# A norm weight moved behind a transposition, and four sums of squares taken in one

## Chip, core and metric

The kernel runs on one core of a Trainium2 chip. The metric is the device time of one execution in microseconds (us). Five engines work side by side, each through a queue of its own that it takes in order: TensorE (PE, with its weight loads shown apart as PEld), VectorE (DVE), ScalarE (ACT), GpSimd (POOL), and SyncE (SP), which here only starts transfers.

## What is computed

The reference is a two-layer transformer trunk over 512 tokens of width 1024. The first layer holds two sparse attentions, the second one differential attention; each layer ends in a multilayer perceptron (MLP). The change lies in the differential attention, in its head-wise norm:

```python
pd = p[:, :, 0] - lam_full * p[:, :, 1]
o = jnp.einsum('bhqs,bshe->bqhe', pd.astype(v.dtype), v)
o = rms_norm(o, subln) * (1.0 - lambda_init)
return o.reshape(B, QBLK, DIFF_HEADS * 2 * DIFF_DIM)
# rms_norm(x, g) = x * rsqrt(mean(x * x, -1) + EPS) * g
```

There are 8 heads, and `o` has 128 values for each head and token; `subln` is a vector of 128 weights that all heads share. Behind the norm an output projection takes all heads together.

## The kernel before

Everything is float32. A product of matrices is made from high and low parts: each operand is split into `hi`, its rounded copy, and `lo`, the rest, and three matmuls (L350 to L352) are added up. A helper writes the split: ACT copies the source into `hi` (L372), DVE subtracts `hi` from the source into `lo` (L373).

`odd()` is the second attention. Its tokens go through in blocks of 128, so that a unit is one head and one block: 32 units, head by head. Each passes through stages that lie some slots apart in one loop: `s0` makes scores and the softmax (DVE L514, ACT L517), `s1` and `s1b` combine the two softmaxes (POOL L1665, DVE L1671), `s2` transposes the result (PE L1681, ACT L531), and `s3` multiplies by the values (PE L1693). The last three are those of the change:

- `s3`, once all four blocks of a head have been multiplied, copies the head's 128x512 result from PSUM to SBUF (ACT L1699) and squares it block by block on ACT, each call also writing the sum of its 128 squares to a column of a small tile `ost` (L1702, the accumulator read being an instruction of its own in the trace). For head 7 this is done after each block, on 128x128, so that the output projection can follow block by block.
- `s4`, one slot later, turns the sums into a factor for each token (DVE L1710, then seven small calls, L384 to L398) and multiplies (DVE L1714): block times factor times weight, `in1=sub`, where `sub` holds the 128 weights on every partition, since the tokens lie on partitions and the weights along the free side.
- `s5`, one more slot later, transposes the blocks (PE L1724) and splits them from PSUM into `hi` and `lo` for the output projection (L372, L373).

Beside the attention, the queries and keys of the next head are projected (`proj_fill`); with head 7 the output projection of heads 0 to 3 runs as filling (`op_unit`), its result added on DVE at L738; heads 4 to 7 follow in `layer()`, with the layer norm (`ln_a_`, L665 to L704, and `ln_b_`, L713 to L724) behind each block of tokens. All this time a stream of weights is loaded and split into parts by ACT (L265) and by DVE or POOL (L266); the weights of the output projection are also multiplied by a gate row (L262, mostly POOL, 128x1024 a call).

The tile `sub` takes one of six buffers of the tag `k`, whose other five hold key tiles of the heads; behind the attention the same buffers serve for weights of the MLP. The order of the instructions on each engine is not written out by hand: `TileContext(nc, schedule_with_timeline_sim=True)` sorts them by simulated readiness, and the loop's order is the priority.

Of the kernel before, what the change touches and what calls it, by code (L numbers as in the profile page):

```python
# [9 lines left out]
F32 = mybir.dt.float32  # L10
F32R = mybir.dt.float32r
I32 = mybir.dt.int32
AF = mybir.ActivationFunctionType
ALU = mybir.AluOpType
AX = mybir.AxisListType
# [13 lines left out]
def f32(ap):  # L29
    return ap.bitcast(F32)  # L30
# [296 lines left out]
class Trunk:  # L327
# [1267 lines left out]
    def odd(self):  # L1595
        nc, a, sm, R, B, C, st, I = self.nc, self.a, self.sm, self.R, self.B, self.C, self.st, self.I
# [1 line left out]
        fill = Fill()  # L1598
        lam = self.z()
        nc.scalar.dma_start(out=lam[:, :256], in_=a["lam"].to_broadcast([128, 256]))  # L1600
        sub = self.s2("k")[:, :128]
        nc.scalar.dma_start(out=sub, in_=a["subln"].to_broadcast([128, 128]))
        lf = sm.tile([128, 4], F32, tag="lf", bufs=1, name="lf")
        self.k_low()

# [17 lines left out]
        for j in range(2):  # L1623
            nc.vector.scalar_tensor_tensor(out=lam[:, 256 + 64 * j:320 + 64 * j], in0=lam[:, 128 * j:128 * j + 64], scalar=1.0,
                                           in1=lam[:, 128 * j + 64:128 * j + 128], op0=ALU.mult, op1=ALU.mult,
                                           accum_out=lf[:, j:j + 1])
# [8 lines left out]
        Q, K, G, ot = {}, {}, {}, []  # L1635
# [49 lines left out]
        def s3(n):  # L1685
            h, i = units[n]
            if i == 0 or h == 7:
                po[h] = self.bank("o", (128, 4, 128))
            pt = pts.pop(n)
            for j in range(i + 1):  # L1690
                js, c = slice(128 * j, 128 * j + 128), 128 * (h % 4)
                v = V[h // 4][j // 2][:, 512 * (j % 2) + c:512 * (j % 2) + c + 128]
                nc.tensor.matmul(po[h][:, i], lhsT=pt[:, js], rhs=v, start=j == 0, stop=j == i)  # L1693
            if i == 3 or h == 7:
                o, sq = self.z(), self.z()
                s = sm.tile([128, 2, 4], F32, tag="ost", bufs=3, name="ost")
                i0 = i if h == 7 else 0
                c = slice(128 * i0, 128 * i + 128)
                nc.scalar.copy(out=o[:, c], in_=po[h].rearrange("p a b -> p (a b)")[:, c])  # L1699
                for i in range(i0, i + 1):  # L1700
                    c = slice(128 * i, 128 * i + 128)
                    nc.scalar.activation(out=sq[:, c], in_=o[:, c], func=AF.Square, accum_out=s[:, 0, i:i + 1])  # L1702
                O[n] = (o, s)

        def s4(n):
            h, i1 = units[n]
            i0 = i1 if h == 7 else 0
            o, s = O[n]
            r = slice(i0, i1 + 1)
            nc.vector.tensor_scalar(out=s[:, 0, r], in0=s[:, 0, r], scalar1=1.0 / 128, scalar2=EPS, op0=ALU.mult, op1=ALU.add)  # L1710
            self.rsqrt(s[:, 1, r], s[:, 0, r], i1 + 1 - i0)
            for i in range(i0, i1 + 1):
                c = slice(128 * i, 128 * i + 128)
                nc.vector.scalar_tensor_tensor(out=o[:, c], in0=o[:, c], scalar=s[:, 1, i:i + 1], in1=sub,  # L1714
                                               op0=ALU.mult, op1=ALU.mult)

        def s5(n):
            h, i1 = units[n]
            i0 = i1 if h == 7 else 0
            o, _ = O.pop(n)  # L1720
            t = self.bank("t")
            for i in range(i0, i1 + 1):
                c = slice(128 * i, 128 * i + 128)
                nc.tensor.transpose(t[:, c], o[:, c], self.ident)  # L1724
            if len(ot) == h:
                ot.append([self.ot() for _ in range(2)])
            c = slice(128 * i0, 128 * i1 + 128)
            self.split(ot[h][0][:, c], ot[h][1][:, c], t[:, c])

        add_proj(0)  # L1730
        fill.flush()
# [3 lines left out]
        for n in range(N + 6):  # L1735
# [12 lines left out]
            if n - 5 in O:  # L1748
                s4(n - 5)
# [4 lines left out]
            if n >= 4 and n - 4 < N:  # L1754
                s3(n - 4)
# [3 lines left out]
            if n - 6 in O:  # L1759
                s5(n - 6)  # L1760
# [93 lines left out]
def onehot(dist):  # L1854
    o = np.zeros((33, len(dist)), np.float32)
    o[np.where(dist < 0, 32, buckets(dist)), np.arange(len(dist))] = 1.0
    return o


def layout(i):  # L1860
    c = np.ascontiguousarray
    i = {k: np.asarray(v) for k, v in i.items()}
    f = {}
    f["x"] = c(i["x"][0])
    f["xT"] = c(i["x"][0].T.reshape(8, 128, 512))
    f["c"] = c(i["c"])
    f["ident"] = np.eye(128, dtype=np.float32)
    rb = i["rel_bias"]
    tab = np.concatenate([rb, rb[:, NSA_SLOTS]], 1)
    f["tab"] = c(np.concatenate([tab, np.full((1, 24), NEG, np.float32)], 0))  # L1870
    dec = 512 - (16 * np.arange(NDEC)[None, :] + 15 - np.arange(16)[:, None])
    f["onehot"] = c(np.concatenate([onehot(511 - np.arange(NVEC)), onehot(dec.ravel())], 1))
    f["cT"] = c(i["c"].reshape(8, 128).T)
    f["ada_w"] = c(i["ada_w"][0, :, :5120].reshape(1024, 40, 128).transpose(1, 2, 0))
    p = i["ada_w"].reshape(2, 2, 4, 128, 24, 256).transpose(0, 4, 1, 3, 2, 5).reshape(96, 128, 1024)
    f["ada_p"] = c(p[40:])
    f["ada_b"] = c(i["ada_b"].reshape(2, 48, 128).transpose(2, 0, 1))
    f["lnc"] = c(np.stack([i["ln_g"], i["ln_b"]]).reshape(2, 4, 8, 128).transpose(3, 0, 1, 2))

    f["ln"] = c(np.stack([i["ln_g"], i["ln_b"]]).reshape(2, 4, 1024))  # L1880
    w = i["ev_w_in"][0]
    q = [w[:, 64 * h:64 * h + 64] for h in range(8)]
    kvc, kvs, kvw, gate, dq, dkv, iq, ik, iw = np.split(w[:, 512:], np.cumsum([256, 256, 256, 24, 512, 128, 512, 64]), 1)

    def b(m):
        n = m.shape[1] // 128
        return m.reshape(8, 128, n, 128).transpose(2, 1, 0, 3)

    f["ev_b1"] = c(np.concatenate([ik, ik, iq[:, :384], kvs[:, 128:], kvw[:, 128:], dkv, gate, iw], 1).reshape(8, 128, 928))
    f["ev_b2"] = c(b(np.concatenate([kvc[:, 128:]] + [q[h] for h in NSA_SLOTS] +  # L1890
                                    [iq[:, 384:], kvs[:, :128], kvw[:, :128], kvc[:, :128]], 1)))
    f["ev_b3"] = c(b(dq))
    f["kv_norm"] = c(i["dsa_kv_norm"].reshape(1, 128))
    f["ukv"] = c(np.concatenate([i["dsa_w_uk"][0].reshape(128, 512), i["dsa_w_uv"][0].reshape(128, 512)], 1))
    pe = np.stack([i["nsa_pe_k"][0], i["nsa_pe_v"][0]])
    f["pe"] = c(pe.reshape(2, 2, 16, 64).transpose(1, 3, 0, 2).reshape(128, 2, 16))
    w1 = np.stack([i["nsa_w1_k"][0], i["nsa_w1_v"][0]])
    f["cmp_w1"] = c(w1.reshape(2, 2, 4, 4, 64, 256).transpose(0, 2, 1, 4, 3, 5).reshape(2, 4, 128, 1024))
    k2, v2 = (m[0].reshape(2, 128, 64).transpose(1, 0, 2) for m in (i["nsa_w2_k"], i["nsa_w2_v"]))
    f["cmp_w2"] = c(np.concatenate([np.concatenate([k2, k2], 2).reshape(128, 256), v2.reshape(128, 128)], 1))  # L1900
    wo = i["ev_w_out"][0].reshape(16, 64, 1024)
    f["ev_out"] = c(wo[NSA_SLOTS + list(range(8, 16))].reshape(8, 128, 1024))
    w = i["od_w_in"][0]
    f["od_qk"] = c(np.stack([b(w[:, :1024]), b(w[:, 1024:2048])], 1))
    f["od_v"] = c(w[:, 2048:].reshape(4, 2, 128, 2, 512).transpose(3, 0, 2, 1, 4))
    f["od_out"] = c(i["od_w_out"][0].reshape(8, 128, 1024))
    f["lam"] = c(i["diff_lam"].reshape(1, 256))
    f["subln"] = c(i["diff_subln"].reshape(1, 128))
    w = np.stack([b(i["mlp_w1"][l]) for l in range(2)])
    w, q = w[:, :6], w[:, 6:].reshape(2, 13, 2, 128, 2, 512)  # L1910
    f["mlp_wp"] = c(np.stack([np.stack([q[:, :, 0, :, 0], q[:, :, 1, :, 1]], 3), np.stack([q[:, :, 1, :, 0], q[:, :, 0, :, 1]], 3)], 2)
                    .reshape(2, 13, 2, 128, 1024))
    f["mlp_w1"] = c(w)
    f["mlp_w2"] = c(i["mlp_w2"].reshape(2, 32, 128, 1024))
    return f
# [14 lines left out]
```

## Time and profile before

| | |
|---|---|
| median of 3 runs | 1438.86 us (1437.71 to 1439.1) |
| the profiled execution | 1441.48 us, its span 1439.4 us |
| PE busy | 1338.4 us (93%) |
| DVE busy | 1141.7 us (79%) |
| ACT busy | 659.8 us (46%) |
| POOL busy | 579.8 us (40%) |
| mean granted clock of TensorE | 0.968 of full speed |

The span runs from the first to the last instruction. The second attention's units lie between some 875 and 1041 us of it; the projection and the norm behind it reach to some 1070 us, and the MLP follows. A busy share is a mean over all stages, so it doesn't say what bounds one of them; the table by stage below does. "Idle before, releaser" names what an engine last waited for. An idle engine costs nothing where another one sets the pace.

### The profile page before, as it was taken

The numbers are of one execution on the slowest core, as the hardware profiler recorded it, in microseconds if no ns is written. First come the engines' busy times: TensorE is split into PE (matmuls) and PEld (weight loads), VectorE is DVE, ScalarE is ACT, GpSimd is POOL, SyncE is SP. The second block draws the span as 40 slices with busy tenths as digits, with TensorE's granted clock in tenths as the row PEclk, the third lists the DMA queues.
The fourth block names the chain that finished last, engine by engine and source line by source line (L and its number), as shares of the span: only waits on it lengthen the run. The fifth ranks groups of instructions, "written<-read, shape, count | busy, mean of one in ns | idle before, by whom it ended". The sixth has DMA issues, their size and how long they took to land.

```text
span 1439.4 us, 22546 instructions
## 1 busy us (share of the span) xinstructions
PE 1338.4 (93%) x8286; PEld 1123.1 (78%) x8286; DVE 1141.7 (79%) x2186; ACT 659.8 (46%) x1412; POOL 579.8 (40%) x432
## 2 busy tenths in 40 slices
PE   6979799998899999999999799999979899999985
PEld 4868676676589888888887687887769789999974
DVE  7778979667569778877789925788976997888898
ACT  3555465746365423333332536776565443333321
POOL 1423577626432444444453721124164533122234
PEclk9989999899999999999999999999989999999997
DMA  9834323313731554544542442332450233323311
GB/s 353 288 116 142 116 89 118 119 58 118 263 117 46 175 191 162 183 169 161 191 161 94 144 164 88 103 103 76 152 163 6 91 100 118 106 72 117 117 59 59
DMA packets 58657, 189.52 MB, mean 132 GB/s; under 512 B 7794, under 2 KB 8498, under 8 KB 58548
## 3 DMA queue, kind: packets, MB, share of 16 engines
q1 hardware_dynamic: 55840, 184.67, 38.0%
q10 hardware_dynamic: 2708, 3.42, 0.7%
q8 instruction: 65, 1.06, 0.3%
q14 instruction: 44, 0.36, 0.1%
HBM read 178.42 MB, written 9.64 MB: 131 GB/s over the span
## 4 chain that ended last, share of the span: by engine, by line
PE 70%; DVE 19%; DMA 4%; issue 3%; ACT 2%; POOL 1%; DVEq 0%; SPq 0%; ACTq 0%; POOLq 0%
PE ps_mm L350 9%; PE ps_mm L351 9%; PE ps_mm L352 9%; PE ps_o L350 4%; PE ps_o L351 4%; PE ps_o L352 4%; PE ps_s L351 3%; PE ps_s L350 3%; PE ps_s L352 3%; PE ps_t L350 2%; PE ps_t L352 2%; PE ps_t L351 2%; PE ps_t L1486 2%; PE ps_s L504 2%; DVE u L738 2%
## 5 line engine op out<-in xcount | busy, mean ns | idle before, releaser
L350 PE MATMUL ps_mm<-hT,b 128*128 128x256 f32 (+1 forms) x560 | 188.9, 339 | 16.9 <-ACT b L265 13.2
L351 PE MATMUL ps_mm<-hT,b 128*128 128x256 f32 (+1 forms) x560 | 188.5, 337 | 5.2 <-DVE hT L724 5.1
L352 PE MATMUL ps_mm<-hT,b 128*128 128x256 f32 (+1 forms) x560 | 187.8, 336 | 1.8 <-DVE b L220 1.8
L350 PEld LDWEIGHTS ps_mm<-hT,b 128*128 128x128 f32 x560 | 107.6, 192 | 31.9 <-ACT b L265 13.2
L351 PEld LDWEIGHTS ps_mm<-hT,b 128*128 128x128 f32 x560 | 107.8, 193 | 17.8 <-DVE hT L724 5.6
L220 POOL TENSOR_TENSOR b<-s,b 128x512 fp32r<-128x512 f32 x33 | 46.6, 1415 | 184.6 <-ACT b L219 181.2
L517 ACT ACTIVATE z<-z,st 128x128 f32<-128x128 f32 (+3 forms) x160 | 89.3, 559 | 67.2 <-DVE st L514 61.3
L903 POOL TENSOR_TENSOR ot<-z,ot 128x512 fp32r<-128x512 f32 x39 | 61.3, 1573 | 142.0 <-ACT ot L902 128.4
L352 PEld LDWEIGHTS ps_mm<-hT,b 128*128 128x128 f32 x560 | 107.5, 192 | 11.4 <-DVE b L220 2.0
L350 PE MATMUL ps_o<-b,ot 128*128 128x512 f32 x251 | 101.2, 403 | 3.9 <-ACT b L265 2.2
L351 PE MATMUL ps_o<-b,ot 128*128 128x512 f32 x251 | 99.5, 397 | 3.0 <-DVE b L266 3.0
L738 DVE TENSOR_TENSOR u<-ps_o,u 128x512 f32<-128x512 f32 x121 | 82.4, 681 | 21.6 <-PE ps_o L352 21.2
L352 PE MATMUL ps_o<-b,ot 128*128 128x512 f32 x251 | 98.8, 394 | 0.0
L514 DVE CUSTOM_DVE_ANT_0 z<-ps_s,g 128x128 f32<-128x128 f32 (+3 forms) x160 | 75.0, 484 | 25.8 <-PE ps_s L505 23.6
L265 ACT CAST b<-raw 128x1024 fp32r<-128x1024 f32 (+1 forms) x62 | 64.5, 1043 | 65.9 <-issue 16.7
L266 DVE TENSOR_TENSOR b<-s,b 128x1024 fp32r<-128x1024 f32 x47 | 70.4, 1501 | 18.3 <-ACT b L265 17.9
L265 ACT CAST b<-s 128x1024 fp32r<-128x1024 f32 x47 | 49.1, 1049 | 77.6 <-DMA s<-mlp_w 18.9
L266 DVE TENSOR_TENSOR b<-raw,b 128x1024 fp32r<-128x1024 f32 (+1 forms) x42 | 56.7, 1349 | 33.1 <-ACT b L265 32.9
L350 PE MATMUL ps_s<-b,ot 128*128 128x512 f32 x181 | 72.4, 400 | 0.0
L738 DVE TENSOR_TENSOR u<-ps_s,u 128x512 f32<-128x512 f32 x87 | 59.3, 682 | 15.9 <-PE ps_s L352 15.6
L351 PE MATMUL ps_s<-b,ot 128*128 128x512 f32 x181 | 71.7, 396 | 0.0
L352 PE MATMUL ps_s<-b,ot 128*128 128x512 f32 x181 | 71.4, 394 | 0.0
(472 smaller groups left out, 4244.1 us busy)
## 6 DMA issues: line engine op xcount, KB each, us to landing
s<-mlp_w SPq DMA_DIRECT2D x55, 512.0 KB
s<-ada_p SPq DMA_DIRECT2D x39, 512.0 KB
s<-mlp_wp SPq DMA_DIRECT2D x33, 512.0 KB
raw<-ada_w SPq DMA_DIRECT2D x23, 512.0 KB
raw<-mlp_w SPq DMA_DIRECT2D x21, 512.0 KB
raw<-mlp_wp SPq DMA_DIRECT2D x19, 512.0 KB
early<-ada_w SPq DMA_DIRECT2D x17, 512.0 KB
raw<-ada_p SPq DMA_DIRECT2D x17, 512.0 KB
```

Source lines behind the costliest of these rows:

```text
L220: (nc.gpsimd if PLAN["sl"][it.l][n] else nc.vector).tensor_tensor(out=lo, in0=src, in1=f32(hi), op=ALU.subtract)
L265: nc.scalar.copy(out=hi.cols(c.start, w), in_=raw[:, c])
L266: getattr(nc, ("vector", "gpsimd")[PLAN["lo"][it.name]] if it.name in PLAN["lo"] else k.lo_engine).tensor_sub(out=lo.cols(c.start, w), in0 ...
L350: mm(ps, lhsT=l[0], rhs=r[0], start=start, stop=False)
L351: mm(ps, lhsT=l[0], rhs=r[1], start=False, stop=False)
L352: mm(ps, lhsT=l[1], rhs=r[0], start=False, stop=stop)
L504: mm(ps, lhsT=q[:, qs], rhs=k[0][:, ks], start=start, stop=False)
L514: i = nc.vector.tensor_tensor_reduce(out=z[:, :w], in0=ps, in1=bias, scale=-1.0, scalar=3e38, op0=ALU.add, op1=ALU.min, accum_out=st[:, m: ...
L517: j = nc.scalar.activation(out=z[:, :w], in_=z[:, :w], func=AF.Exp, scale=-1.0, bias=st[:, m:m + 1], accum_out=st[:, 2 + m:3 + m])
L738: self.nc.vector.tensor_add(out=u[:, sl], in0=ps, in1=u[:, sl])
L903: (nc.gpsimd if PLAN["hl"][l][f % 2] else nc.vector).tensor_tensor(out=hl[:, c0:c1], in0=r[:, c0:c1], in1=f32(hh[:, c0:c1]), op=ALU.subtract)
L1486: self.nc.tensor.transpose(t[:, 128 * j:128 * j + 128], z[:, 128 * j:128 * j + 128], self.ident)
```

## The change

The weight becomes a factor for each partition. It is loaded as a 128x1 tile of its own instead of a row on all partitions (the array that the kernel gets is reshaped to match), `s4` multiplies by the token's factor alone, and the weight is applied behind the transposition in `s5`, where the 128 positions of a head lie on partitions: ACT writes `hi` with the weight as its scale, DVE writes `lo` as source times weight minus `hi`. In `s3` the four squares with accumulators become one ACT call on 128x512 without, and DVE sums its four blocks in one reduction; for head 7, where this goes block by block, it is a call on 128x128 and a reduction to 128x1 for each.

```diff
-        sub = self.s2("k")[:, :128]
-        nc.scalar.dma_start(out=sub, in_=a["subln"].to_broadcast([128, 128]))
+        sub = sm.tile([128, 1], F32, tag="sub", bufs=1, name="sub")
+        nc.scalar.dma_start(out=sub, in_=a["subln"])
...
-                for i in range(i0, i + 1):
-                    c = slice(128 * i, 128 * i + 128)
-                    nc.scalar.activation(out=sq[:, c], in_=o[:, c], func=AF.Square, accum_out=s[:, 0, i:i + 1])
+                nc.scalar.activation(out=sq[:, c], in_=o[:, c], func=AF.Square)
+                nc.vector.reduce_sum(out=s[:, 0, i0:i + 1], in_=sq[:, c].rearrange("p (a b) -> p a b", b=128), axis=AX.X)
...
-                nc.vector.scalar_tensor_tensor(out=o[:, c], in0=o[:, c], scalar=s[:, 1, i:i + 1], in1=sub,
-                                               op0=ALU.mult, op1=ALU.mult)
+                nc.vector.tensor_scalar(out=o[:, c], in0=o[:, c], scalar1=s[:, 1, i:i + 1], scalar2=None, op0=ALU.mult)
...
-            self.split(ot[h][0][:, c], ot[h][1][:, c], t[:, c])
+            hi, lo = (x[:, c] for x in ot[h])
+            nc.scalar.activation(out=hi, in_=t[:, c], func=AF.Identity, scale=sub)
+            nc.vector.scalar_tensor_tensor(out=lo, in0=t[:, c], scalar=sub, in1=f32(hi), op0=ALU.mult, op1=ALU.subtract)
...
-    f["subln"] = c(i["diff_subln"].reshape(1, 128))
+    f["subln"] = c(i["diff_subln"].reshape(128, 1))
```

## Rows read from the trace of the kernel before

**Rows 1.** The page: its head line.

```profile
span 1439.4 us, 22546 instructions
```

**Rows 2.** Busy us by stage: length, PE, PEld, DVE, ACT, POOL, clock, DMA.

```profile
920.00:940.00 20.00, 20.00 (x109) 16.75 (x108) 16.12 (x50) 15.51 (x42) 2.46 (x4) 1.00 0.26 80
960.00:980.00 20.00, 19.73 (x109) 16.73 (x108) 16.74 (x44) 13.86 (x39) 9.89 (x8) 1.00 0.40 109
980.00:1000.00 20.00, 17.60 (x100) 14.27 (x98) 18.68 (x49) 16.04 (x51) 8.46 (x7) 1.00 0.37 105
...
1020.00:1040.00 20.00, 19.15 (x96) 14.92 (x94) 19.84 (x68) 12.35 (x27) 2.48 (x1) 1.00 0.50 171
1040.00:1060.00 20.00, 13.32 (x65) 10.84 (x65) 18.04 (x37) 12.68 (x25) 12.59 (x10) 0.95 0.39 145
1060.00:1080.00 20.00, 15.88 (x104) 15.18 (x105) 13.17 (x20) 12.78 (x31) 10.21 (x7) 0.71 0.71 207
```

**Rows 3.** Waits, 960 to 1070 us: in total, times, longest us.

```profile
PE ps_t L713 <- ACT ot L719: 7.2, 2, 6.9
...
PE ps_mm L350 <- DVE u L738: 2.9, 3, 2.1
...
PE ps_t L1724 <- DVE z L1714: 1.3, 1, 1.3
...
DVE ost L1710 <- ACT z L1702: 1.0, 2, 0.6
```

**Rows 4.** Groups by line, 880 to 1060 us: count, busy us, mean ns.

```profile
L1702 ACT ACTIVATE z<-z 128x128 f32<-128x128 f32 x32 | 9.5, 299 | 0.3
...
L1702 ACT ACTIVATION_READ_ACCUMULATOR z<-z 128x1 f32 x32 | 6.0, 187 | 0.0
...
L373 DVE TENSOR_TENSOR ot<-ps_t,ot 128x512 fp32r<-128x512 f32 x7 | 4.8, 679 | 0.5 <-ACT ot L372 0.5
```

**Rows 5.** The chain that ended last, 880 to 1090 us: start, us, what.

```profile
996.25 1.29 ACT z L1702 x8
```

**Rows 6.** Nearest to the new calls: timeline, min/median/max by line, groups by form.

```profile
283.19 0.35 DVE L1416 TENSOR_SCALAR z<-z,st,one 128x128 f32<-128x128 f32 x1
...
L1547 DVE TENSOR_SCALAR z<-z x2: 215/854/1494, 123.0 to 157.9; 128x124 f32<-128x124 f32 x2
...
L1242 DVE TENSOR_REDUCE cst<-z x8: 256/273/285, 139.7 to 232.9; 128x4 f32<-128x128 f32 x8
...
L265 ACT CAST k<-raw 128x512 fp32r<-128x512 f32 x14 | 8.7, 622 | 18.7 <-PE ps_t L351 8.9 <-issue 4.6 <-DMA raw<-mlp_w 2.4
...
L372 ACT CAST ot<-ps_t 128x128 fp32r<-128x128 f32 x4 | 0.9, 263 | 0.1
...
L719 ACT ACTIVATE ot<-ps_t,lnr 128x128 f32<-128x128 f32 x88 | 31.9, 464 | 4.3 <-PE ps_t L713 4.3
...
L373 DVE TENSOR_TENSOR ot<-ps_t,ot 128x128 fp32r<-128x128 f32 x3 | 0.8, 284 | 0.0
```

**Rows 7.** DVE in order of time, 960 to 1041 us: start, us.

```profile
972.18 1.14 DVE L1714 SCALAR_TENSOR_TENSOR z<-z,ost,k 128x128 f32<-128x128 f32 x4
...
997.56 2.39 DVE L1710 TENSOR_SCALAR ost<-ost 128x4 f32<-128x4 f32 x1 [0.60 <-ACT z L1702]
...
1009.48 3.27 DVE L1714 SCALAR_TENSOR_TENSOR z<-z,ost,k 128x128 f32<-128x128 f32 x4
...
1018.41 0.16 DVE L1710 TENSOR_SCALAR ost<-ost 128x4 f32<-128x4 f32 x1
...
1040.90 0.35 DVE L1714 SCALAR_TENSOR_TENSOR z<-z,ost,k 128x128 f32<-128x128 f32 x1
```

**Rows 8.** POOL in order of time, the same stretch.

```profile
997.57 2.36 POOL L262 TENSOR_TENSOR raw<-raw,grow 128x1024 f32<-128x1024 f32 x1
...
1009.58 2.50 POOL L262 TENSOR_TENSOR raw<-raw,grow 128x1024 f32<-128x1024 f32 x1 [0.60 <-DMA raw<-od_out]
```

**Rows 9.** ACT in order of time, 1016 to 1068 us; idle before.

```profile
1041.28 0.62 ACT L265 CAST k<-raw 128x512 fp32r<-128x512 f32 x1 [0.77 <-DVE z L1714]
```

## The prediction, made before the changed kernel was run

> **What bounds the kernel now.** I read five views, from the whole to the place. The page gives the span of the profiled execution [rows 1]. The table by stage comes next, for the stretch in which the second attention runs and ends [rows 2]: up to about 980 us TensorE (PE) is full (20.00 of 20 us, then 19.73), while VectorE (DVE) has three to four us in twenty to spare. From 980 us it turns round: DVE is busy 18.68 of 20 us, then 19.84, then 18.04, and PE falls to 13.32 between 1040 and 1060. After that PE runs at a mean granted clock of 0.71 of full speed for 20 us. So what is added to DVE before 980 us lies beside a full PE, and what is added behind it is in the way.
>
> The list of waits says for whom PE waits in 960 to 1070 us [rows 3]: 7.2 us for ScalarE's (ACT) L719, which belongs to the layer norm behind the attention; 2.9 us for DVE's L738, which empties a bank of the output projection; 1.3 us for L1714, a line that the change rewrites. DVE in turn waits 1.0 us in two places at L1710 for ACT's squares at L1702, a wait that the change moves to its new sum.
>
> The groups by line and form give the lines touched [rows 4], one line's share of the chain stands beside them [rows 5], the nearest instructions to the new ones have rows of their own [rows 6], and DVE's order of time shows a second thing [rows 7]: four calls of L1714 take 1.14 us at 972 us but 3.27 us at 1009 us, and one L1710 on 128x4 takes 2.39 us at 997.56 where it takes 0.16 at 1018.41. In both long cases GpSimd (POOL) is in a 128x1024 product at that moment [rows 8]. A DVE call that reads or writes SBUF while such a product runs can lose some 2.2 us, and where each lands is a matter of order.
>
> **The change part by part.**
>
> The squares. Per head 0 to 6 ACT loses four L1702 calls of 299 ns with four accumulator reads of 187 ns [rows 4]. They overlap: the eight fill 1.29 us in the chain of waits [rows 5]. It gains one 128x512 square without accumulator. No row shows it; the nearest is ACT's 128x512 cast from SBUF at 622 ns [rows 6], and I take that. ACT frees about 0.7 us for each head. ACT has 12 to 16 of 20 us in this stretch [rows 2], so I count the freed time at nothing; it counts only in the latency of the chain, below.
>
> The sum. DVE gains one 128x512 to 128x4 reduction for each of seven heads, and a 128x128 to 128x1 one for each of the four units of head 7. The small one has a near row, 273 ns for 128x128 to 128x4 [rows 6]. For the large one I add the slope between DVE's 128x128 and 128x512 forms of L373, 284 and 679 ns [rows 4, 6]: 0.27 + 0.40 = 0.67 us. If it ran at two elements a cycle, the slope would be halved: 0.47. Calls in a row overlap by 0.08 us (four of 0.35 fill 1.14 [rows 7]), so in line it is 0.59 (0.39 to 0.67), and 0.19 (up to 0.27) for the small one.
>
> The normalisation. Thirty-two L1714 calls with two tensors become tensor-times-scalar calls with one. A clean L1714 takes 0.35 us [rows 7]. The nearest rows for the new one are L1416, 128x128 with two per-partition scalars, 0.35 us, and L1547, 128x124 with constants, 0.215 us at its shortest [rows 6]. The new call has one scalar, so I take the middle, 0.28. That saves 0.07 a call (0 to 0.13), 0.27 a head.
>
> The split behind the transposition. DVE's L373 becomes a form with a per-partition scalar. I bound its price by what a scalar costs in the row above (0.35 against 0.215 for two, so 0.07 each), from 0 to 0.10. ACT's L372 gets a scale from a tile: L719 with two such operands takes 464 ns, L372 of the same shape and source 263 ns [rows 6], so 0.10 for one, beside other work except in the very last unit, where the missing accumulator read gives it back.
>
> The rest. The weight's load becomes one number per partition instead of a row on all; it is issued some hundred us before its use, the scaling by a constant shrinks from 128x128 to 128x1, both nothing. The weight also no longer holds a buffer of the tag "k". One MLP weight cast waits 0.77 us for the last reader of that buffer, L1714 [rows 9]. Without it ACT would be free earlier, but its next work there, the last L372, waits for the same L1714 through the transposition. I count nothing.
>
> The sum. A head costs DVE 0.59 - 0.27 + 0.07 = +0.4 us (from -0.12 = 0.39 - 0.51 + 0 up to 0.78 = 0.67 - 0 + 0.10, rounded); a unit of head 7 costs 0.19 - 0.07 + 0.07 = +0.2 us (0.06 to 0.37). Over the kernel that is 7 x 0.4 + 4 x 0.2 = 3.6 us of DVE. Heads 0 to 3 are summed before 980 us beside a full PE; that cover hides them, and without it they would cost 1.6 more. Heads 4 to 6 and head 7 stand in the tight stretch: 3 x 0.4 + 4 x 0.2 = +2.0. Against it stands the 1.0 us in which DVE waits for the squares: ACT's shorter chain (0.62 against 1.29) lets the sum begin some 0.7 us earlier, so it fills that idle time. What was late next, L1710, then follows on DVE itself. Net: +1.0 us.
>
> The profiled execution took 1441.48 us, 1439.4 of it span, and is 2.6 us above the median of the three runs, 1438.86. The sum gives 1442.5 beside that one and 1439.9 beside the median; I forecast the median.
>
> **A rule beside the rows.** That a DVE call is held up for as long as a POOL product lasts is what [rows 7, 8] show for calls with two SBUF inputs and for a tiny tensor-times-scalar. The Trainium skill, page "SBUF — State Buffer", section "Who interferes with whom", states that a reduction on this chip never takes the pair of ports that DVE shares with GpSimd, while the one-tensor scalar form does when its operands meet the conditions of the faster mode. By that rule the new sums could lie under a POOL product for nothing, and the rewritten L1714 is as exposed as it was. The eight reductions in this trace, 256 to 285 ns [rows 6], show no delayed one, which fits. The rule is a reason for the faster rival below: if three sums fell under products, 1.8 us of the sum above would vanish.
>
> **The rivals.**
>
> *Faster: the order falls well.* The instructions of each engine are laid out by a planner that follows durations, so everything behind the first changed call may come in another order. Two of the 2.2 us collisions go (L1710 at 997 us and L1714 at 1009 us), and the last unit's L1714, which runs at 1040.90 and keeps PE waiting 1.3 us, comes earlier. 1438.86 + 1.0 - 4.4 - 1.3 = about 1434. For it: most of POOL's long products already hit a DVE call, so there is little left to get worse. Against: nothing in the change aims at it, and the number of exposed calls stays.
>
> *Slower: the longer DVE queue comes up behind one more POOL product in 1016 to 1067 us.* DVE is at 19.84 of 20 us there and everything that PE waits for comes through it. The place is the last units of head 7 with the sums in front of each; the price is the upper bounds of the DVE terms for heads 4 to 7, 3 x 0.78 + 4 x 0.37 = 3.8, with the 1.0 us not regained, plus one collision of 2.2 us or part of it: 1443.5 to 1444.9, say 1444. It decides from the point where the last L1714 comes later than now by more than PE's remaining projection covers, since PE then starts the MLP later by all of it, and it does so in a stretch where its granted clock is already down.
>
> *The change does nothing to the time:* the DVE terms end at their lower bounds, -0.12 x 3 + 0.06 x 4 - 1.0 = -1.1, so 1437.7. This and the forecast cannot be told apart by a clock.
>
> **How the numbers follow.** The forecast with its own bounds (1437.7 to 1442.7, the lower from the paragraph above, the upper 1438.86 + 3.8 with no wait regained) has 0.42; the faster order 0.28, about 1434; the slower one 0.30, about 1444. A measurement here tells some 0.2% from no change, 2.9 us, so faster means under 1436.0 and slower over 1441.7. The forecast's band reaches a little over 1441.7 and the faster rival a little into the middle, which leaves 0.28, 0.41 and 0.31. To hold eight in ten the range goes from 1433.5 to 1445.5: a good half us beyond the farther ends of the two rivals.
>
> **What would show it.** In the profile after: the large sums near 0.67 us, the scalar calls near 0.28, L1702 gone as a pair and 0.62 as one call; DVE's total up by 3 to 4 us, ACT's down by about that; the wait for the squares at the sum gone or short; the last normalisation within a us or two of 1041 us; PE's waits at L713 unchanged. The forecast is wrong if DVE's collisions with POOL's 128x1024 products change in number, if the weights' low parts (L266) are laid differently between the last units and the norm, or if the sum runs at twice or half the price taken.

## The result and the profile after

| | before | after |
|---|---|---|
| median | 1438.85 us (1437.71 to 1439.1) | 1446.78 us (1444.31 to 1448.78) |
| ratio of after to before | | 1.0054 (95%: 1.0038 to 1.0069) |
| measured again | 1440.85 us | 1444.76 us, 1.0021 (1.0004 to 1.0038) |
| the profiled execution, its span | 1441.48, 1439.4 us | 1446.03, 1444.2 us |

The change makes the kernel slower, by 4 us in the second measurement (12 runs, beside 35 of the kernel before) and by 8 in the first (4 runs each). 1439.9 was forecast, in a range that ended at 1445.5; the second median, 1444.76, lies within it, but beside 1440.85 for the kernel before.

The page of the changed kernel, its head and the busy time of the engines:

```profile
span 1444.2 us, 22511 instructions
...
PE 1338.5 (93%) x8286; PEld 1122.3 (78%) x8286; DVE 1143.3 (79%) x2197; ACT 656.6 (45%) x1359; POOL 577.9 (40%) x432
```

DVE has 1.6 us more than before, ACT 3.2 less. The groups by line and form, 880 to 1060 us, that answer to [rows 4] (count, busy us, mean ns, idle before):

```profile
L1713 DVE TENSOR_SCALAR z<-z,ost 128x128 f32<-128x128 f32 x32 | 7.4, 288 | 0.1
...
L1728 DVE SCALAR_TENSOR_TENSOR ot<-ps_t,sub,ot 128x512 fp32r<-128x512 f32 x7 | 5.2, 748 | 0.8 <-ACT ot L1727 0.7
...
L1701 DVE TENSOR_REDUCE ost<-z 128x4 f32<-128x512 f32 x7 | 4.8, 680 | 0.6 <-ACT z L1700 0.6
L1700 ACT ACTIVATE z<-z 128x512 f32<-128x512 f32 x7 | 4.4, 630 | 0.2
...
L1727 ACT ACTIVATE ot<-ps_t,sub 128x128 fp32r<-128x128 f32 x4 | 1.3, 362 | 2.0 <-PE ps_t L1722 2.0
L1728 DVE SCALAR_TENSOR_TENSOR ot<-ps_t,sub,ot 128x128 fp32r<-128x128 f32 x4 | 1.3, 339 | 0.0
...
L1701 DVE TENSOR_REDUCE ost<-z 128x1 f32<-128x128 f32 x4 | 1.0, 271 | 0.0
```

So the new instructions cost about what was forecast one by one. The table by stage, columns as in [rows 2], shows where the time went:

```profile
980.00:1000.00 20.00, 16.46 (x91) 13.35 (x91) 18.75 (x49) 14.58 (x34) 7.68 (x7) 0.99 0.32 88
1000.00:1020.00 20.00, 20.00 (x101) 17.07 (x100) 16.14 (x49) 7.96 (x22) 6.17 (x5) 0.92 0.14 41
1020.00:1040.00 20.00, 17.25 (x82) 13.55 (x81) 17.11 (x68) 11.27 (x26) 3.19 (x2) 0.91 0.51 184
1040.00:1060.00 20.00, 17.87 (x76) 14.22 (x74) 15.41 (x40) 13.08 (x26) 9.49 (x8) 0.91 0.37 128
1060.00:1080.00 20.00, 11.29 (x75) 10.27 (x74) 10.25 (x20) 13.53 (x30) 11.01 (x9) 0.74 0.47 161
```

Before, DVE had 19.84 and 18.04 busy us in the stretches from 1020 to 1060, and PE's granted clock was 1.00 up to 1040 [rows 2]. Now DVE has 17.11 and 15.41, and the clock is down from 1000 on. DVE isn't simply fuller here, both engines wait for each other. The wait of DVE for PE, 960 to 1070 us, before and after (us, times, longest):

```profile
DVE u L738 <- PE ps_mm L352: 1.6, 3, 0.9
```

```profile
DVE u L738 <- PE ps_mm L352: 7.0, 6, 1.9
```

**How the stage is measured.** Ahead of this place two executions of one program differ: the first L1671, with which the second attention begins, starts at 878.5 us in one trace of the changed kernel and at 873.6 in another, and between 871.9 and 882.9 in all traces of this study. Behind it they agree to 2.1 us: from the start of the last L724 (the end of the norm behind the attention) to the end of the span it is 352.8 to 354.9 us in all of them. So the stage from the first L1671 to the last L724 is compared by itself. Its row before, columns as in [rows 2]:

```profile
879.30:1086.00 206.70, 189.65 (x1055) 161.06 (x1054) 167.22 (x448) 141.22 (x373) 65.07 (x56) 0.97 0.36 111
```

and after:

```profile
878.50:1090.40 211.90, 193.11 (x1055) 163.69 (x1054) 167.01 (x458) 138.57 (x320) 63.44 (x56) 0.95 0.34 108
```

The stage is 5.2 us longer, though DVE, third of the busy columns, works no longer in it than before (167.01 and 167.22 us). PE idles 18.79 us in it (211.90 less 193.11) instead of 17.05, which is 1.7; and the same 1055 matmuls keep it busy 3.5 us longer. The second part is the clock. PE alone in stretches of 4 us, after (length, busy, matmuls, clock):

```profile
996.00:1000.00 4.00, 1.91 (x11) 0.96 0.58 180
1000.00:1004.00 4.00, 4.00 (x16) 0.62 0.31 68
1004.00:1008.00 4.00, 4.00 (x23) 1.00 0.36 131
...
1024.00:1028.00 4.00, 3.31 (x22) 1.00 0.41 128
1028.00:1032.00 4.00, 2.79 (x16) 1.00 0.40 124
1032.00:1036.00 4.00, 3.48 (x12) 0.72 0.98 382
...
1044.00:1048.00 4.00, 1.87 (x8) 0.93 0.89 315
1048.00:1052.00 4.00, 4.00 (x13) 0.64 0.49 168
```

Three times PE stands idle for some 2 us (at 1024 to 1032 in pieces) and then works for 3 to 4 us at the lower of its two levels (1.2 GHz), 13 or 16 matmuls in a full stretch where 23 fit. Summed over stretches of 1 us, busy time times one less the clock, each time costs 1.7 us, 5.1 in all. Behind PE's long wait for the norm (L713, from 1056 us on) the lower level cost 3.8 us before and costs 2.4 now, which leaves some 3.7 us, about the 3.5 found. The trace of before has a clock of 1.00 from 996 to 1056 us, behind its waits too:

```profile
1000.00:1004.00 4.00, 2.81 (x12) 1.00 0.00 2
...
1040.00:1044.00 4.00, 2.42 (x10) 1.00 0.85 306
```

The first of the three falls stands behind no line of the change. PE waits 2.1 us there for a call of L1671 that a POOL product, from 996.64 to 998.99 us, holds; before, such a product held an L1710 [rows 7]:

```profile
996.92 2.49 DVE L1671 SCALAR_TENSOR_TENSOR z<-z,st 128x384 f32<-128x384 f32 x1
```

Before, PE waits as long at this place, for L738 [rows 3], and the clock stays up; in a second trace of the changed kernel it falls again, but in one of the old order (p0, in the last section) it falls too. So some 1.7 us of the 5.2 may be chance.

The other two falls: what PE waits for between 1023.5 and 1056.5 us, after (us, times, longest):

```profile
PE ps_t L1722 <- DVE z L1713: 3.0, 2, 1.9
PE ps_mm L350 <- DVE u L738: 1.4, 3, 0.8
PE ps_mm L350 <- ACT ot L1727: 0.5, 1, 0.5
```

The first is the rewritten normalisation. DVE in order of time tells why it is late for head 6:

```profile
1021.68 0.74 DVE L1671 SCALAR_TENSOR_TENSOR z<-z,st 128x512 f32<-128x512 f32 x1
1022.34 0.87 DVE L1701 TENSOR_REDUCE ost<-z 128x4 f32<-128x512 f32 x2
...
1023.53 0.16 DVE L391 TENSOR_TENSOR t<-yi 128x4 f32<-128x4 f32 x1
1023.89 1.23 DVE L266 TENSOR_TENSOR b<-raw,b 128x1024 fp32r<-128x1024 f32 x1 [0.19 <-ACT b L265]
1025.03 2.35 DVE L391 TENSOR_TENSOR t<-yi 128x1 f32<-128x1 f32 x1
1027.30 0.15 DVE L392 TENSOR_TENSOR t<-t,ost 128x4 f32<-128x4 f32 x1
...
1028.12 1.21 DVE L266 TENSOR_TENSOR b<-s,b 128x1024 fp32r<-128x1024 f32 x1
...
1029.39 1.21 DVE L266 TENSOR_TENSOR b<-s,b 128x1024 fp32r<-128x1024 f32 x1
...
1031.34 1.05 DVE L1713 TENSOR_SCALAR z<-z,ost 128x128 f32<-128x128 f32 x5
```

The steps on 128x4 belong to head 6. Three splits of weights and a call that a POOL product holds for 2.35 us stand between them, so that they take from 1022.3 to 1032. Before, the same steps were through ahead of the splits and of the held call:

```profile
1021.21 1.14 DVE L1714 SCALAR_TENSOR_TENSOR z<-z,ost,k 128x128 f32<-128x128 f32 x4
...
1023.05 1.23 DVE L266 TENSOR_TENSOR b<-raw,b 128x1024 fp32r<-128x1024 f32 x1
1024.19 2.35 DVE L396 SCALAR_TENSOR_TENSOR t<-t 128x1 f32<-128x1 f32 x1
```

The planner has laid out this stage anew. The last normalisation moves in the same way, from 1040.90 [rows 7] to 1045.77 us.

### The profile page after: what moved, and what is told of

Read it like the earlier page. It is cut to its first block, busy times and chain, and to the rows that moved or that the text cites. A ratio compares the mean times of both kernels' runs of the same rounds, so it can differ in the third digit from the quotient of the medians.

```text
span 1444.2 us, 22511 instructions
## 1 busy us (share of the span) xinstructions
PE 1338.5 (93%) x8286; PEld 1122.3 (78%) x8286; DVE 1143.3 (79%) x2197; ACT 656.6 (45%) x1359; POOL 577.9 (40%) x432
## 4 chain that ended last, share of the span: by engine, by line
PE 64%; DVE 21%; DMA 5%; issue 4%; ACT 4%; POOL 2%; DVEq 0%; ACTq 0%; POOLq 0%; SPq 0%
PE ps_mm L350 8%; PE ps_mm L351 8%; PE ps_mm L352 8%; PE ps_o L350 4%; PE ps_o L351 4%; PE ps_o L352 4%; PE ps_s L351 3%; PE ps_s L350 3%; PE ps_s L352 3%; PE ps_t L352 2%; PE ps_t L350 2%; PE ps_t L351 2%; DVE u L738 2%; DVE b L266 2%; PE ps_s L504 1%
## 5 line engine op out<-in xcount | busy, mean ns | idle before, releaser
L738 DVE TENSOR_TENSOR u<-ps_o,u 128x512 f32<-128x512 f32 x121 | 82.3, 680 | 22.5 <-PE ps_o L352 22.2
L514 DVE CUSTOM_DVE_ANT_0 z<-ps_s,g 128x128 f32<-128x128 f32 (+3 forms) x160 | 75.3, 484 | 23.1 <-PE ps_s L505 20.7
L266 DVE TENSOR_TENSOR b<-raw,b 128x1024 fp32r<-128x1024 f32 (+1 forms) x42 | 56.9, 1355 | 33.2 <-ACT b L265 32.9
L266 DVE TENSOR_TENSOR b<-s,b 128x1024 fp32r<-128x1024 f32 x47 | 67.3, 1436 | 18.7 <-ACT b L265 18.4
L738 DVE TENSOR_TENSOR u<-ps_s,u 128x512 f32<-128x512 f32 x87 | 59.2, 681 | 15.6 <-PE ps_s L352 15.3
```

The source lines that it names most:

```text
L266: getattr(nc, ("vector", "gpsimd")[PLAN["lo"][it.name]] if it.name in PLAN["lo"] else k.lo_engine).tensor_sub(out=lo.cols(c.start, w), in0 ...
L514: i = nc.vector.tensor_tensor_reduce(out=z[:, :w], in0=ps, in1=bias, scale=-1.0, scalar=3e38, op0=ALU.add, op1=ALU.min, accum_out=st[:, m: ...
L738: self.nc.vector.tensor_add(out=u[:, sl], in0=ps, in1=u[:, sl])
```

## The experiments

Two theories: the stage is longer because DVE has more to do (the theory of the work, W in the expectations), or because the planner, fed with other durations, laid the queues out in another order (the theory of the order, O). The last three columns are of one trace each: the stage as above, PE busy in it, and the difference of the two.

| run | median, us | ratio to before (95%) | stage | PE busy | idle |
|---|---|---|---|---|---|
| before | 1438.9 to 1441.7 | 1 | 206.7 | 189.65 | 17.1 |
| after | 1446.78 | 1.0054 (1.0038 to 1.0069) | 211.9 | 193.11 | 18.8 |
| a1_changed_again | 1444.76 | 1.0021 (1.0004 to 1.0038) | 211.9 | 193.00 | 18.9 |
| e1_squares | 1442.91 | 1.0019 (1.0001 to 1.0037) | 210.2 | 191.36 | 18.8 |
| e2_weight | 1445.69 | 1.0038 (1.0020 to 1.0055) | 216.9 | 193.46 | 23.4 |
| f1_after_edge | 1442.84 | 1.0009 (0.9994 to 1.0024) | 210.7 | 193.44 | 17.3 |
| f2_before_edge | 1439.29 | 0.9993 (0.9976 to 1.0010) | 207.1 | 189.97 | 17.1 |
| p0_old_work_old_order | 1441.75 | 1.0000 (0.9982 to 1.0018) | 207.8 | 190.83 | 17.0 |
| p1_new_work_old_order | 1441.85 | 1.0010 (0.9987 to 1.0032) | 210.9 | 191.70 | 19.2 |
| p1_again | 1441.92 | 1.0006 (0.9982 to 1.0031) | 210.9 | 191.63 | 19.3 |
| p2_old_work_new_order | 1445.87 | 1.0024 (1.0004 to 1.0044) | 212.0 | 192.16 | 19.8 |
| p2_again | 1444.91 | 1.0021 (1.0001 to 1.0042) | 213.1 | 192.36 | 20.7 |
| n1_head6_early | 1447.78 | 1.0033 (1.0010 to 1.0056) | 213.5 | 192.53 | 21.0 |
| n2_both_early | 1446.35 | 1.0039 (1.0021 to 1.0058) | | | |
| n4_before_last_early | 1440.71 | 1.0001 (0.9978 to 1.0024) | 208.5 | 190.86 | 17.6 |
| h1_new_order_first_part | 1443.40 | 1.0018 (1.0001 to 1.0035) | 211.2 | 191.46 | 19.7 |
| h2_new_order_two_parts | 1444.84 | 1.0028 (1.0009 to 1.0047) | 211.8 | 192.03 | 19.8 |
| h3_new_order_last_part | 1442.67 | 1.0013 (0.9999 to 1.0028) | 210.6 | 191.84 | 18.8 |

The three programs that were traced twice give the same stage to within 1.1 us, as do the kernel before and p0, which is that kernel with its own order written out. Idle time repeats better (0.1 us, in p2 0.9) than the part that the clock adds, where one fall more or less makes 1.7 us. (The trace of n2 has a granted clock of 0.95 where PE is full, so its stage is left out and only its waits are read.)

### Each half of the change alone

The squares and sums alone, with the weight left where it was:

```diff
-                for i in range(i0, i + 1):
-                    c = slice(128 * i, 128 * i + 128)
-                    nc.scalar.activation(out=sq[:, c], in_=o[:, c], func=AF.Square, accum_out=s[:, 0, i:i + 1])
+                nc.scalar.activation(out=sq[:, c], in_=o[:, c], func=AF.Square)
+                nc.vector.reduce_sum(out=s[:, 0, i0:i + 1], in_=sq[:, c].rearrange("p (a b) -> p a b", b=128), axis=AX.X)
```

> Only the squares are changed (one ACT call per head, then DVE's sum); the weight stays a row in front of the transposition. Theory W (the added DVE work in the tight stretch is what costs): this half holds all of the added work, 3 x 0.6 + 4 x 0.2 = 2.6 us of DVE there, so it should carry most of the loss, 1443 us or more. Theory O (the order costs: in the changed kernel PE has five fillings of the output projection queued ahead of the last transpositions of head 6, before it had four): here the instruction list has four, so the loss should be small, 1439 to 1442.

And the weight behind the transposition alone, with the squares as they were:

```diff
+        sub = sm.tile([128, 1], F32, tag="sub", bufs=1, name="sub")
...
+                nc.vector.tensor_scalar(out=o[:, c], in0=o[:, c], scalar1=s[:, 1, i:i + 1], scalar2=None, op0=ALU.mult)
...
+            nc.scalar.activation(out=hi, in_=t[:, c], func=AF.Identity, scale=sub)
+            nc.vector.scalar_tensor_tensor(out=lo, in0=t[:, c], scalar=sub, in1=f32(hi), op0=ALU.mult, op1=ALU.subtract)
```

> Only the weight is moved behind the transposition; the squares with their accumulators stay. Theory W: DVE has less to do here (-0.27 + 0.07 us per head), so 1438 to 1439 us. Theory O: the instruction list has five fillings ahead of head 6's last transpositions, as in the changed kernel, so 1443 to 1448.

Both are slower than before. e1's 1442.91 us lies between what the two theories gave, e2's 1445.69 where the theory of the order had it. In the stage the one with less work on DVE is the slower (in the whole time their intervals overlap): the weight's half takes time from DVE (0.07 us less for each of 32 calls, 0.06 to 0.07 more for each of eleven) and has the longest stage of all, 216.9 us. Time doesn't follow DVE's work. Neither run is in the order of the kernel before, since the planner laid out both anew.

### One edge of the order

In the new order PE does five fillings of the output projection ahead of head 6's last transposition (L1681) instead of four. In the changed kernel the fifth was bound to come behind it:

```diff
+AFTER = {4: 27}
...
+                if k in AFTER:
+                    stack.enter_context(self.tc.issue_after(tr[AFTER[k]]))
+                self.op_unit(oo, ot, u, t, half)
```

> The changed kernel with one edge of order: the fifth filling of the output projection may not be issued on PE before the last transposition of head 6. No work is added or removed. Theory W: nothing moves, 1444 to 1448 us. Theory O: head 6's norm comes some 4 us earlier than in the changed kernel, PE's idle gaps behind 1024 us shrink, 1438 to 1442.

and in the kernel before the transposition was bound to come behind five fillings:

```diff
+            fill.run(4 * 2600 if n == 29 else amount * (1 - 0))
...
+                    if n == 29:
+                        stack.enter_context(self.tc.issue_after(last[4]))
```

> The kernel before, with the same order forced the other way: head 6's last transpositions wait on PE behind the fifth filling. No work is added or removed. Theory W: 1438 to 1440 us. Theory O: this alone makes the kernel before slower, 1442 to 1447.

Forced on the old kernel this edge costs nothing (207.1 us); taken from the new one it leaves 210.7, and a whole time (1.0009) that can't be told from before. (f1's 1442.84 us lies between what the two theories gave, f2's 1439.29 where the theory of the work had it.) What f1 gains back is idle time (17.3 us), but PE is as long busy as in the changed kernel, its clock being down as much. So the edge isn't what costs. Neither run moves it alone: the planner laid out what follows anew. In f2's trace DVE's calls stand in another order than before in some 30 places from 128 us of the stage on, as many as in h3 below, head 7's last L1714 comes 3 us later, and nothing is lost. A new order by itself need not cost.

### Work and order crossed

Here the order of every queue is written out, and only the order: the old work in the new order, the new work in the old, the old in the old as control, and the changed kernel as it is.

```diff
         Trunk(tc, aps, out).run()
+        queue_up(tc)
...
+def queue_up(tc):
+    by = {i.name: i for i in tc.nc.cur_bb.bb.instructions}
+    for seq in ORDER.values():
+        names = [f"I-{n}" for n in seq if f"I-{n}" in by]
+        for p, q in zip(names, names[1:]):
+            tc.add_manual_dep(by[q], p, info, reason="written order")
```

The new order is the one planned for the changed work with the weight's tile left in its buffer of tag `k`, since the old work needs that buffer; apart from a handful of places (of L713, L723, L724 and L266 above all) it is the changed kernel's.

> The changed kernel's instructions in the order of the kernel before, written out for every engine (the one square takes the place of a head's last, the sum stands in front of L1710's successor). The times from the first L1671 to the last L724 are 206.7 us in the trace of before and 211.9 in that of the changed kernel. Theory W (the work): 210 to 212 here. Theory O (the planner's new order): 206 to 208, and about 1.0 to 1.001 of the kernel before in whole.

> The instructions of the kernel before in the changed kernel's order, written out for every engine (four squares where the one stood, the sums left out). Theory W: 206 to 208 us from the first L1671 to the last L724. Theory O: 210 to 213, and 1.003 to 1.006 of the kernel before in whole.

> The control for both: the kernel before with its own order written out, the same instructions in the same places. Both theories: the time of the kernel before, a ratio within 0.2% of one, and 206 to 208 us from the first L1671 to the last L724. If it is not, the writing out costs something itself, or the stage varies by more than I think.

> The changed kernel once more, beside the others on the same chip. Both theories: 1.003 to 1.007 of the kernel before, and 211 to 213 us from the first L1671 to the last L724. If it comes out within 0.2% of the kernel before, the first result was a matter of the chip's state.

The control p0 came out as expected. The changed kernel's second ratio, 1.0021, is less than expected and just over the 0.2% named there; its stage, 211.9 us, is that of the first trace.

Old work in the new order, PE in the stage:

```profile
877.50:1089.50 212.00, 192.16 (x1055) 0.96 0.34 108
```

That is as slow as the changed kernel, in the whole time (1.0024 and 1.0021 beside 1.0021 of a1) and in the stage. The new order alone, with not one instruction changed, is enough to lose as much, if a little less than the 1.003 expected. The new work in the old order:

```profile
871.90:1082.80 210.90, 191.70 (x1054) 0.96 0.33 109
```

In the whole time it can't be told from before (1.0010 and 1.0006). In the stage it does cost 3.1 to 4.2 us, so the work has a price too. The two don't add up: 3.1 to 4.2 for the work, 4.2 to 6.4 for the order, 4.1 to 5.2 for both. In the stage each theory's own run came out as that theory had it (p1 in 210 to 212, p2 in 210 to 213) and against the other: either is enough for most of the loss, and neither can be called its cause to the exclusion of the other.

> The new work in the order of the kernel before, a second time, to tell whether its 210.9 us for the stage (ratio 1.001) repeats. If the work itself costs about what the prediction's bounds gave (1.0, up to 3.8 us), the stage is again 208.5 to 211.5 and the ratio 1.000 to 1.003; if 210.9 was an accident of the clock in one execution, it is 207 to 208.

### The late normalisations moved

Head 6's steps were put together ahead of the splits of weights, on DVE alone, the other queues as they were:

```diff
 L391 TENSOR_TENSOR t<-yi 128x4
+L392, L393, L394, L396, L397, L398 on 128x4, L1713 x4
 L266 TENSOR_TENSOR b<-raw,b 128x1024
 L391 TENSOR_TENSOR t<-yi 128x1
-L392 TENSOR_TENSOR t<-t,ost 128x4
...
-L1713 TENSOR_SCALAR z<-z,ost 128x128 x4
```

> The changed kernel with its own order on every engine, but on DVE the seven small steps and four multiplications of head 6's normalisation stand together, ahead of the 2.35 us collision with POOL and of three splits of weights (L266), between which the planner had put them. Theory 'place': in the changed kernel these steps began 3 us later than before (at +143.8 us behind the first L1671, not some +139) and so fell behind that collision and those splits, which stretched them to +153.9; PE then waited and its clock fell. It expects the normalisation at about +148 (one step may still be held by the POOL product), the ninth L738 at +155 to +157 instead of +159.3, and the stage from the first L1671 to the last L724 at 208 to 210 us instead of 211.9; ratio 1.000 to 1.003. Rival 'work': the stage is longer because of what DVE does, wherever it stands: 211.9 us again, ratio about 1.004.

n2 does the same, and puts L396, L397, L398 and L1713 of the last unit ahead of two L738 and seven L266:

> As the run before, and the last unit's four final steps (L396, L397, L398, L1713) also stand together, ahead of two L738 and seven L266 between which the planner had put them. 'Place' expects the last normalisation some 6 us earlier (about +157 instead of +167.3), no wait of PE for it (1.9 us in the changed kernel), no fall of PE's clock behind it, and the stage at 205 to 208 us; ratio 0.998 to 1.001. If the last unit's place costs nothing, the stage is that of the run before.

My theory of the place fell. The steps came where they should: head 6's normalisation began at 146.7 us of the stage instead of 152.8, the last one in n2 at 159.3 instead of 167.3. Nothing got shorter, 213.5 us in n1 and a ratio of 1.0039 in n2. PE's waits in the same 33 us, n1 (its two longest):

```profile
PE ps_t L1722 <- DVE z L1713: 2.5, 1, 2.5
PE ps_mm L351 <- DVE b L266: 2.3, 1, 2.3
```

and n2:

```profile
PE ps_mm L350 <- DVE u L738: 3.2, 2, 2.2
PE ps_mm L351 <- DVE b L266: 2.9, 1, 2.9
```

In n2 the wait for the normalisation is gone, and waits for the split weights and for emptied banks have come in its place. Most of PE's waits here are for DVE, and in these runs what goes ahead in that queue makes something else late that PE wants just as soon.

The counterpart on the kernel before, its last unit's four steps moved forward in the same way:

> The kernel before with its own order, but the last unit's four final steps (L396, L397, L398, L1714) stand together ahead of two L738 and seven L266. 'Place' expects the last normalisation at about +155.5 instead of +161.6, PE's wait of 1.3 us for it gone, and the stage 1 to 2 us shorter than 206.7 to 207.8, so 205 to 206.5; ratio 0.998 to 1.000. If PE's own queue sets the end there, the wait only moves to the next L738 and the stage stays at 206.7 to 207.8.

The last normalisation came 5 us earlier (156.6 instead of 161.6 us) and the stage didn't get shorter (208.5; 1.0001). The wait moved to L738 here too (2.7 us in place of 1.3 and 0.8). None of these three beats the kernel before.

### The new order in parts

The orders differ in blocks that can be exchanged one by one. With the old work, the new order was taken up to head 6's first transpositions (h1), up to the end of head 7's softmaxes (h2), only from there on (h3), and in whole:

> The work of the kernel before. The instructions stand in the order of the changed kernel up to the first transpositions of head 6's probabilities on PE (some 105 to 110 us behind the first L1671), and from there on in the order of the kernel before. If the part that costs is the first one (heads 4 to 6, where DVE and ACT change places of softmaxes and projections of the next head), the stage is 210 to 213 us and the ratio 1.002 to 1.004; if it is one of the later ones, the stage is 206.5 to 208.5 and the ratio 0.998 to 1.002.

> The same with the new order kept up to the end of head 7's softmaxes (a fifth filling of the output projection ahead of head 6's last transposition, the last softmaxes behind more fillings), and the old order only for the last units' normalisations, fillings and norm. If it is the middle part that costs, since fillings that ran early are missing later beside a chain that came later, the stage is 210 to 213 us and the ratio 1.002 to 1.004, where the run before has 206.5 to 208.5. If the last part costs, it is still 206.5 to 208.5.

> The work of the kernel before, in the old order up to the end of head 7's softmaxes, and from there on in the new one: the small steps of head 6 and of head 7's first block between three splits of weights, and the norm's steps behind. If the last part costs, 210 to 213 us and 1.002 to 1.004; if the first two do, 206.5 to 208.5 and 0.998 to 1.002.

> The work of the kernel before in the whole new order, a second time, beside the three parts: 211 to 213 us for the stage and a ratio of 1.001 to 1.005, as the first time (212.0 us, 1.0024). If the first time was an accident, 206.5 to 208.5 and 1.000.

No part is the one that costs. The first alone gives 211.2, the last alone 210.6, two together 211.8, all 212.0 and 213.1: each of these departures from the old order loses some 3 to 4.5 us in the stage and the next ones little more. In the whole time h3 (1.0013) can't be told from before.

## Why the prediction was wrong

**The prices were right.** The large sum took 680 ns (0.67), the small one 271 (0.27), the scalar call 278 in the median (0.28), the square 0.63 us (0.62), the split with a scalar 748 instead of 679 ns and 339 instead of 284 (+0.07), ACT's 362 instead of 263 (+0.10). ACT came down by 3.2 us. DVE rose by 1.6 us only, not by 3 to 4; the calls that POOL products hold lost some 1.4 us less (below), the rest of the difference I can't place. The wait for the squares went from 1.0 to 0.6 us, not to nothing.

**The cover of heads 0 to 3** held in the new order only. In the first 100 us of the stage PE idles 1.7 us after and 1.8 before (98.33 and 98.20 us busy). In the old order, for which the sum was made, it is 3.0: PE waits 0.7 us for L473, the low half of the next head's queries, and 0.3 for L1713. The sum had these 1.2 us at nothing.

**The sum.** +1.0 us was meant for the order as it was. The run that measures this, p1, gives 0.9 and 1.4 us in the whole time, which fits but has an interval of some 3.5 us to either side; in the stage it gives 3.1 to 4.2, the upper end of my bounds (3.8) or a little over. 2.2 us of that are idle time (19.2 against 17.0 or 17.1 us): 1.2 from the cover and 1.0 behind it, where the sum had its 1.0. The rest, 0.9 us beside p0 and 2.0 beside the trace of before, is the same matmuls at the lower level of the clock, which the sum left out.

**The step that failed** is the one from DVE's added time to the kernel's time. The sum passes it on one for one, +2.0 less the 1.0 regained, in the order as it was, and has PE's clock at nothing. The runs show in its place that PE's waits grew by about what the sum allowed (1.7 us after) and that the same 1055 matmuls then took 3.5 us longer (2.3 beside p0), since PE ran at the lower level behind its waits. More than half of what the stage lost is this. I had read the lower clock at 1060 to 1080 us [rows 2] as part of the scenery; it is a price that a long wait of PE can carry, up to nearly doubling it, and it belonged into the sum and into each rival.

The order was mispriced as well. I gave a new one two outcomes of about equal chance, some 5 us faster or 5 us slower, and counted both in collisions with POOL's products and in the last normalisation. The number of collisions did not change: each of the four POOL products from 985 to 1030 us holds one DVE call, after (1.23, 2.49, 1.37 and 2.35 us) as before (1.34, 2.39, 3.27 and 2.35), and what they took was less. What changed is whom they hold: the second one holds the L1671 that PE waits for. The last normalisation did come 5 us later, but n2 and n4 show that moving it alone gains nothing. So the slower rival's 1444, near the 1444.76 of the second measurement, is near by luck: its mechanism, one more collision and the last normalisation behind it, isn't what the traces show. The prediction's own sign of being wrong, splits (L266) laid differently between the last units and the norm, was there.

Nor was the coin a fair one. Ten programs with another order or other work, in thirteen traces, have a stage of 210.2 to 216.9 us; before, p0, n4 and f2, all with the old work, have 206.7 to 208.5. In idle time alone nine of the ten lie at 18.8 us or more, f1 at 17.3, and the four at 17.0 to 17.6. None of the ten gained, which speaks against 0.28 for a faster order; but f2, whose order is also new, lost nothing. [rows 2] gave a hint of this: DVE at 19.84 of 20 us with PE at 19.15 leaves little slack into which something could be moved.

**What the profile after would show**: the large sums, scalar calls and squares did; L713's wait rose from 7.2 to 8.2 us instead of staying; the last normalisation missed its bounds by 3 us.

**What stays open.** Why most departures cost about the same, and f2's none, is not settled: no single block, edge or chain carries it. How much of the 5.2 us is the work's and how much the order's stays open too, since either alone loses nearly as much. That the new order comes from the changed durations of the calls fits the queues (on DVE nearly all differences lie behind the first changed call of the attention) but isn't shown. Which duration turned it wasn't tried; the freed buffer of tag `k` does little, as the order planned without it is the changed kernel's in nearly all places.

## What to carry to other kernels

Where queues are laid out by a planner, a change of a few call prices is two changes: the work, and an order for the whole stage behind it. Measure them apart, the old work in the new order and the new work in the old one, before explaining a difference by the instructions that were edited. In a stage where two engines feed each other without slack, price a wait of TensorE with the clock that it can lose behind it (here 1.7 us a time), and expect a step that is moved forward to make another one late.

## What the runs showed of the hardware

**The clock after a gap is not settled by the gap.** In the trace of p0, whose queues are those of before, PE (busy, matmuls, clock):

```profile
1000.00:1004.00 4.00, 2.21 (x6) 0.78 0.07 27
1004.00:1008.00 4.00, 4.00 (x20) 0.79 0.05 13
```

PE waits 2.1 us for the same L738 as in the trace of before [rows 3], and the clock falls behind it to the lower level for 3 to 4 us; before, it didn't fall. That alone is 1.7 us between two executions of one order. In the traces of this study (without n2's), between 80 us of the stage and the norm, 2 of 17 waits of 1.2 to 1.65 us were followed by a fall and 19 of 28 waits of 1.8 to 3.0 us. The Trainium skill, page "TensorE: Matmul & The Clock Gate", section "HAM oscillation — how this bites in real kernels", describes the same pattern, a wait for data that drops the clock so that the next tile starts slow, and gives some 1.67 us at the lower rate for each; its waits are for DMA and some 3 to 5 us long. The traces agree in kind, not in size: here waits of about 2 us for VectorE can be enough, and the stretches at the lower level are 3 to 4 us long and cost 1.7 us each.

**A POOL product and DVE.** n1 has the four rewritten multiplications under one, DVE and then POOL:

```profile
1029.59 2.98 DVE L1713 TENSOR_SCALAR z<-z,ost 128x128 f32<-128x128 f32 x4
```

```profile
1029.51 2.38 POOL L266 TENSOR_TENSOR b<-raw,b 128x1024 fp32r<-128x1024 f32 x1 [3.40 <-ACT b L265]
```

2.98 us instead of 0.88, so the one-tensor scalar call is held as the two-tensor one was. In p1 a sum runs into a product, and the next call is held:

```profile
990.56 0.69 DVE L1701 TENSOR_REDUCE ost<-z 128x4 f32<-128x512 f32 x1 [0.22 <-ACT z L1700]
991.28 2.06 DVE L1709 TENSOR_SCALAR ost<-ost 128x4 f32<-128x4 f32 x1
```

The product began at 990.94 us, inside the sum, which took its usual 0.69 us; the 128x4 call behind it ended with the product, at 993.3. This agrees with the rule of the Trainium skill weighed in the prediction (page "SBUF — State Buffer", section "Who interferes with whom"). It is no full test, since the sum had begun first. The trace of before has two on 128x128 that began under a product. One is the first of the eight L1242 that the prediction read [rows 6]; POOL and then DVE:

```profile
138.96 2.69 POOL L266 TENSOR_TENSOR b<-early,b 128x1024 fp32r<-128x1024 f32 x1 [2.51 <-ACT b L265]
```

```profile
139.67 0.27 DVE L1242 TENSOR_REDUCE cst<-z 128x4 f32<-128x128 f32 x1
```

It took 0.27 us and was through while the product ran on to 141.65; the other, L1249 at 231.37 us, took 0.28 under a product from 229.56 to 231.97. So these two reductions were not held. A sum on 128x512 that begins under a product occurs in no trace here.
